# A hybrid decoder step on one core: convolution blocks earlier and further apart, LayerNorm beside the last projections

## Chip, core and metric

The kernel runs on one core of one Trainium2 chip. The metric is the time of one execution in microseconds (us); 3151.36 is the median of three. A profile is one execution recorded by the hardware profiler. Engines are called PE (matrix products), DVE (vector), ACT (activations, scalar engine), POOL (GpSimd) and SP (sync engine, which issues most DMAs).

## The reference, cut

One layer over 2048 prompt rows and 32 sample rows (2080 columns in the kernel, which works on transposed data). All branches come from one projection of the normalized input:

```python
h = _rmsnorm(x, g_pre) @ w_in
qa, ka, va, za, ub, zb, qc, zc, gt = jnp.split(h, SPLITS, axis=-1)
...                                                # A: dilated attention of qa, ka, va
glu = ub[..., :EB] * jax.nn.sigmoid(ub[..., EB:])   # B: EB = 768
full = jnp.concatenate([hist_conv, glu], axis=1)
conv = lax.conv_general_dilated(full, conv_w[:, None, :], ..., feature_group_count=EB) + conv_b
ob = jax.nn.silu(_layernorm(conv, ln_g, ln_b))      # width 31; norm over 768 channels
...                                                # C: cross-attention of qc into 256 memory rows
mix = (gates[..., 0, :] * ((oa * jax.nn.silu(za)) @ w_pa)
       + gates[..., 1, :] * ((ob * jax.nn.silu(zb)) @ w_pb)
       + gates[..., 2, :] * ((oc * jax.nn.silu(zc)) @ w_pc))
y = x + _rmsnorm(mix @ w_out, g_post)
```

## The kernel before

**Stages.** First x is loaded, normalized and transposed in six groups of columns (`stage_x`), split into a high and a low part (x0h, x0l and so on), and two weight blocks q0 and q1 are multiplied chunk by chunk as x arrives. Then come the other projections of this stage, one block for each 128 output columns. A block loads its weights (`load_w`), splits them on POOL into `whi` and `wlo` (L55, L56), and runs 144 matmuls on PE into the PSUM tile `g` (L166 to L168): 6 chunks of columns (384 wide, then 256 and 288) by 8 row blocks by 3 products. Then the memory stage (`memory`: keys and values of the memory rows, the LayerNorm, cross-attention), the sample's attention, the prompt's attention, and a last stage that projects the branches and the output. A further set of projections (za, zb, zc, gt; PSUM tile `gg`) has low priority and fills gaps of PE from the end of the first projections until after attention; it is called the filler below.

**Blocks.** k and v blocks copy chunks to `st` (ACT), transpose them on PE and copy them to `ro` on DVE (L260, L264) for the outputs. q and qc blocks only store `st`. A u block is two weight blocks: the gate (tanh on ACT into `gate`) and the values, whose chunks DVE joins with the gate into `G` (prompt) and `GS` (sample) at L298 and L303. The order before is u0, k0, k1, k2, u1, k3, k4, k5, u2 and so on: each u with three others, q2 to q5 and qc0 to qc3 among the last.

**Convolution.** After each u block, `conv` takes 31 taps on DVE: L313 writes the accumulator `acc` (one buffer), L322 adds the other taps, L331 and L333 handle the sample. Then `acc` is stored to `d_c` (L335, SP). It is put off by 900 in priority (`later(LAG)`), so that it fills DVE beside the blocks that follow.

**LayerNorm.** `conv_norm` is a generator with one step for each of 9 chunks of 256 columns: load from `d_c` (L663), sum over six channel blocks (L665, DVE), sum over partitions by a product with `ones` on PE (L667, tile `str`), subtraction (L668), squares on ACT (L671), their sum (L673), again a product (L675, tile `sco`), variance (L677), root, scaling (L679, and POOL at L681), tanh on ACT (L684), product (L685), store. `memory_kv` takes a step after each of its eight weight blocks. The norm has pools of its own there.

**Order.** A scheduler gives each engine one fixed instruction order from priorities, its own estimates of times, and free buffers. On the chip every engine takes its list strictly in order, and waits at an instruction whose inputs are not there.

Of the kernel before, what the change touches and what calls it, by code (L numbers as in the profile page):

```python
# [7 lines left out]
F32 = mybir.dt.float32  # L8
R32 = mybir.dt.float32r
AF = mybir.ActivationFunctionType  # L10
ALU = mybir.AluOpType
# [14 lines left out]
LAG = 900  # L26
EARLY = 1
IN_COLS = 9472

# [8 lines left out]
class K:  # L38
# [134 lines left out]
    def phase_a1(self, wp, blocks=None):  # L173
        tc, nc, I, O = self.tc, self.nc, self.I, self.O
        with tc.tile_pool(name="x12", side="right", bufs=1) as xpool, \
                tc.tile_pool(name="stg", side="right", bufs=3) as stg, \
                tc.tile_pool(name="sm1", side="right", bufs=2) as small, \
                tc.tile_pool(name="wr", side="right", bufs=2) as self.wr, \
                tc.tile_pool(name="psg", side="right", bufs=4, space=PSUM, reuse_waits="tile") as psg, \
                tc.tile_pool(name="pst", side="right", bufs=3, space=PSUM, reuse_waits="tile") as pst:  # L180
            for th in (1, 2):
                n = THIRDS[th][1]
                self.X[th] = tuple([xpool.tile([128, n], R32, name=f"x{th}{c}{k}") for k in range(8)]
                                   for c in "hl")
            with tc.tile_pool(name="xst", side="right", bufs=7) as xst:
                st = self.stage_x(xst, small, pst)
                next(st)
                self.consts(self.cpool, xst, pst)
                ws = [self.load_w(wp, self.win(CQ), 8, rp=self.wr)]
                for _ in st:  # L190
                    pass
            with tc.tile_pool(name="brw", side="right", bufs=1) as bp:
                self.taps(self.cpool, bp, pst)
                self.bias_rows(self.cpool, bp, pst)

            out = [(th, c, k) for th in (1, 2) for c in range(2) for k in range(8)]

            with tc.tile_pool(name="cnv", side="right", bufs=1, reuse_waits="tile") as cnv:
                ws.append(self.load_w(wp, self.win(CQ + 128), 8, rp=self.wr))
                for cs, js in [(c, j) for c in (CHUNKS[:1], CHUNKS[1:2], CHUNKS[2:3], CHUNKS[3:4], CHUNKS[4:]) for j in range(2)]:  # L200
                    for s, n in cs:
                        self.chunk("q", js, s, n, ws[js], stg, psg, "g", pst)
                order = []
                rest = [("k", j) for j in range(6)] + [("v", j) for j in range(6)] + \
                       [("q", j) for j in range(2, 6)] + [("qc", j) for j in range(4)]
                for j in range(6):
                    order += [("u", j)] + rest[:3]
                    rest = rest[3:]
                order += rest
                for kind, j in order:  # L210
                    if blocks is not None and (kind, j) not in blocks:
                        continue
                    if kind == "u":
                        gs = self.blk_u(j, wp, stg, cnv, psg, pst)
# [7 lines left out]
                assert not out  # L222
                self.early = {("za", j): self.load_w(wp, self.win(CZA + 128 * j), 8, rp=self.wr) for j in range(EARLY)}
    def blk_x(self, kind, j, wp, stg, psg, pst):
# [42 lines left out]

    def blk_u(self, j, wp, stg, cnv, psg, pst):
        nc, I, O = self.nc, self.I, self.O
        G = cnv.tile([128, 16, 130], F32, name="G", bufs=2)  # L270
        GS = cnv.tile([128, 8, 34], F32, name="GS", bufs=2)
        nc.gpsimd.memset(G[:, :, 0:2], 0.0)
# [7 lines left out]
        for x in range(2):  # L280
            nc.vector.tensor_scalar(GS[:, 4 * x:4 * x + 4, 0:30],
                                    p[:, x * 128:x * 128 + 120].rearrange("p (b w) -> p b w", b=4),
                                    2.0, None, op0=ALU.mult)

        w = self.load_w(wp, self.win(CUB + EB + j * 128), 8, rp=self.wr)
        gate = cnv.tile([128, T], F32, name="gate")
# [5 lines left out]
        for s, n in CHUNKS:  # L292
            th = gate[:, s:s + n]
            pa = psg.tile([128, 512], F32, name="g")
            self.gemm(pa[:, :n], w, [self.x_at(k, s, n) for k in range(8)])
            m = min(n, S - s)
            r0 = s // 128
            nc.vector.scalar_tensor_tensor(G[:, r0:r0 + m // 128, 2:130],  # L298
                                           th[:, :m].rearrange("p (r i) -> p r i", i=128), 1.0,
                                           pa[:, :m].rearrange("p (r i) -> p r i", i=128),  # L300
                                           op0=ALU.add, op1=ALU.mult)
            if m < n:
                nc.vector.scalar_tensor_tensor(GS[:, :, 30:34],  # L303
                                               th[:, m:n].rearrange("p (b t) -> p b t", t=4), 1.0,
                                               pa[:, m:n].rearrange("p (b t) -> p b t", t=4),
                                               op0=ALU.add, op1=ALU.mult)
        return G, GS

# [345 lines left out]

    def conv_norm(self, lp, ps):
        nc = self.nc
        ones = lp.tile([128, 128], F32, name="ones")
        nc.vector.memset(ones, 1.0)
        W = 256
        for s in range(0, T, W):  # L660
            n = min(W, T - s)
            x = lp.tile([128, 6, W], F32, name="c", bufs=3)[:, :, :n]
            nc.sync.dma_start(x, self.d_c[:, :, s:s + n].rearrange("j p n -> p j n"))  # L663
            sm = lp.tile([128, W], F32, name="sm", bufs=2)[:, :n]
            nc.vector.tensor_reduce(sm, x.rearrange("p j n -> p n j"), axis=AX.X, op=ALU.add)  # L665
            p = ps.tile([128, 512], F32, name="str")[:, :n]
            nc.tensor.matmul(p, ones, sm, start=True, stop=True)  # L667
            nc.vector.scalar_tensor_tensor(x, p[:, None, :].to_broadcast([128, 6, n]), -1.0 / EB, x,  # L668
                                           op0=ALU.mult, op1=ALU.add)
            sq = lp.tile([128, 6, W], F32, name="sq", bufs=1)[:, :, :n]  # L670
            nc.scalar.activation(sq, x, AF.Square)  # L671
            sm = lp.tile([128, W], F32, name="sm", bufs=2)[:, :n]
            nc.vector.tensor_reduce(sm, sq.rearrange("p j n -> p n j"), axis=AX.X, op=ALU.add)  # L673
            p = ps.tile([128, 512], F32, name="sco")[:, :n]
            nc.tensor.matmul(p, ones, sm, start=True, stop=True)  # L675
            var = lp.tile([128, W], F32, name="var")[:, :n]
            nc.vector.tensor_scalar(var, p, 1.0 / EB, EPS, op0=ALU.mult, op1=ALU.add)  # L677
            rs = self.rsqrt(lp, var, [128, W], "ln", n)
            nc.vector.tensor_tensor(x, x, rs[:, None, :].to_broadcast([128, 6, n]), op=ALU.mult)  # L679
            for j in range(6):  # L680
                nc.gpsimd.tensor_scalar(x[:, j], x[:, j], self.v("ln_g", j), self.v("ln_b", j),  # L681
                                        op0=ALU.mult, op1=ALU.add)
            t = lp.tile([128, 6, W], F32, name="sq", bufs=1)[:, :, :n]
            nc.scalar.activation(t, x, AF.Tanh, scale=0.5)  # L684
# [199 lines left out]
    def memory(self):  # L884
        tc = self.tc
        with tc.tile_pool(name="mem", side="right", bufs=1, reuse_waits="tile") as kp, \
                tc.tile_pool(name="ln", side="right", bufs=1, reuse_waits="tile") as lp, \
                tc.tile_pool(name="lnp", side="right", bufs=1, space=PSUM, reuse_waits="tile") as lps:
            ln = self.conv_norm(lp, lps)
            with tc.tile_pool(name="mem1", side="right", bufs=1, reuse_waits="tile") as mp, \  # L890
                    tc.tile_pool(name="mem1p", side="right", bufs=2, space=PSUM, reuse_waits="tile") as ps, \
                    tc.tile_pool(name="memw", side="right", bufs=2, reuse_waits="tile") as wp:
                KT, VV = self.memory_kv(mp, kp, wp, ps, ln)
            for _ in ln:
                pass
            with tc.tile_pool(name="mem2", side="right", bufs=1, reuse_waits="tile") as mp, \
# [7 lines left out]

    def memory_kv(self, mp, kp, wp, ps, ln):
        nc, I, O = self.nc, self.I, self.O
# [22 lines left out]
        for c in range(8):  # L929
# [18 lines left out]
            if c >= 4:  # L948
# [3 lines left out]
                VV.append((vh, vl))  # L952
            next(ln, 0)
        return KT, VV
# [353 lines left out]
```

## Time and profile before

| | |
|---|---|
| median of 3 runs (lowest to highest) | 3151.36 us (3148.8 to 3155.62) |
| the profiled execution, its own time | 3154.4 us |
| its span in the profile | 3152.6 us |
| mean granted clock of PE | 0.979 |
| PE, DVE, POOL, ACT busy | 3000.2, 2014.8, 1350.4, 1124.2 us |
| first projections end (last matmul into `g`) | 868.6 us |
| filler (matmuls into `gg`) | 868.7 to 2549.7 us |
| starts of the six convolutions | 154.1, 274.0, 394.2, 514.4, 634.6, 754.9 us |

The page gives, for each engine, busy time and its share of the span; the chain that ended last; and groups of instructions by line. Since each engine works in order, one asks in each stretch which engine is never idle, and, where PE is idle, what it waited for.

### The profile page before, as it was taken

How to read it: one execution, taken by the hardware profiler on the slowest of the kernel's cores; microseconds unless marked ns; L12 is line 12 of the kernel's file. 1: busy time of each engine (PE TensorE's matmuls, PEld its weight loads, DVE VectorE, ACT ScalarE, POOL GpSimd, SP SyncE). 2: the span in 40 equal slices, each digit the busy share in tenths (PEclk: the TensorE clock that was granted, in tenths of full speed). 3: DMA queues.
4: the chain of work that ended last, by engine and by line, in shares of the span. 5: the costliest groups of instructions: out<-in, count | busy, mean ns of one | idle time of the engine just before them, and what ended most of it. 6: DMA issues, size and time to landing. Idle time of an engine off the chain costs nothing.

```text
span 3152.6 us, 55374 instructions
## 1 busy us (share of the span) xinstructions
PE 3000.2 (95%) x20705; PEld 2839.9 (90%) x20705; DVE 2014.8 (64%) x3734; ACT 1124.2 (36%) x2835; POOL 1350.4 (43%) x1048
## 2 busy tenths in 40 slices
PE   7999999999987999999999999989899979999998
PEld 6899999999987999998999999989898967787897
DVE  5297797796677926465546766666656457556563
ACT  5010010010132433243437575656565523222221
POOL 0121221142356537444256565667676433233240
PEclk9899999999999999999999999999999989999999
DMA  7232222211265454477454656576555487657561
GB/s 250 85 103 80 80 60 61 63 62 50 81 182 167 135 153 144 147 219 239 151 139 116 161 123 163 128 185 150 156 143 152 109 279 227 223 168 227 161 197 53
DMA packets 532218, 454.66 MB, mean 144 GB/s; under 512 B 118191, under 2 KB 458581, under 8 KB 531137
## 3 DMA queue, kind: packets, MB, share of 16 engines
q1 hardware_dynamic: 357502, 335.36, 36.2%
q10 hardware_dynamic: 169840, 105.02, 11.7%
q0 software_dynamic: 4608, 10.75, 1.2%
q8 instruction: 164, 2.69, 0.4%
q14 instruction: 104, 0.85, 0.1%
HBM read 332.96 MB, written 118.04 MB: 143 GB/s over the span
## 4 chain that ended last, share of the span: by engine, by line
PE 70%; DMA 12%; DVE 7%; issue 4%; POOL 3%; ACT 2%; SPq 1%; ACTq 0%; DVEq 0%; POOLq 0%
PE g L166 8%; PE g L167 8%; PE g L168 8%; PE gg L166 6%; PE gg L168 6%; PE gg L167 6%; PE pg L168 3%; PE pg L166 3%; PE pg L167 3%; PE pt L571 2%; DMA cb<-d_cf 2%; PE y L1180 2%; PE y L1179 2%; PE y L1178 2%; PE o L598 1%
## 5 line engine op out<-in xcount | busy, mean ns | idle before, releaser
L166 PE MATMUL gg<-x0h,whi 128*128 128x256 f32 (+1 forms) x2560 | 747.9, 292 | 25.9 <-DVE st L246 12.2
L168 PE MATMUL gg<-x0h,wlo 128*128 128x256 f32 (+1 forms) x2560 | 741.8, 290 | 0.1
L167 PE MATMUL gg<-x0l,whi 128*128 128x256 f32 (+1 forms) x2560 | 741.1, 290 | 0.0
L55 POOL TENSOR_SCALAR whi<-wraw 128x1024 fp32r<-128x1024 f32 x162 | 242.7, 1500 | 928.5 <-PE g L167 524.1
L166 PEld LDWEIGHTS gg<-x0h,whi 128*128 128x128 f32 x2560 | 493.2, 193 | 35.0 <-DVE st L246 13.7
L167 PEld LDWEIGHTS gg<-x0l,whi 128*128 128x128 f32 x2560 | 493.5, 193 | 2.2 <-issue 0.5
L168 PEld LDWEIGHTS gg<-x0h,wlo 128*128 128x128 f32 x2560 | 493.2, 193 | 2.2 <-POOL wlo L56 0.3
L322 DVE SCALAR_TENSOR_TENSOR acc<-G,cw,acc 128x1536 f32<-128x1536 f32 (+15 forms) x354 | 480.8, 1408 | 0.3
L56 POOL TENSOR_TENSOR wlo<-wraw,whi 128x1024 fp32r<-128x1024 f32 x162 | 417.0, 2575 | 9.4 <-PE gg L168 0.2
L155 POOL TENSOR_TENSOR clo<-craw,chi 128x768 fp32r<-128x768 f32 (+1 forms) x96 | 174.1, 1815 | 346.0 <-ACT chi L154 329.8
L627 ACT ACTIVATE P<-T,stm 128x128 f32<-128x128 f32 (+1 forms) x576 | 260.8, 455 | 141.0 <-DVE stm L625 94.8
L239 ACT ACTIVATE st<-g 128x384 f32<-128x384 f32 (+1 forms) x132 | 60.2, 461 | 570.7 <-PE g L168 550.7
L166 PE MATMUL pg<-ac,chi 128*128 128x512 f32 (+1 forms) x640 | 229.4, 359 | 16.6 <-ACT chi L154 8.7
L625 DVE CUSTOM_DVE_ANT_0 T<-s,bias 128x128 f32<-128x128 f32 (+1 forms) x576 | 191.5, 357 | 80.8 <-PE s L617 47.0
L167 PE MATMUL pg<-ac,chi 128*128 128x512 f32 (+1 forms) x640 | 228.8, 358 | 6.3 <-DVE ac L1198 6.3
L168 PE MATMUL pg<-ac,clo 128*128 128x512 f32 (+1 forms) x640 | 227.6, 357 | 3.6 <-POOL clo L155 3.6
L576 DVE TENSOR_TENSOR pl<-pt,ph 128x512 fp32r<-128x512 f32 x240 | 155.6, 652 | 52.4 <-ACT ph L575 48.9
L168 PE MATMUL g<-x0h,wlo 128*128 128x384 f32 x544 | 184.3, 339 | 2.9 <-POOL wlo L56 2.9
L166 PE MATMUL g<-x0h,whi 128*128 128x384 f32 x544 | 183.6, 338 | 2.6 <-ACT st L239 2.3
L167 PE MATMUL g<-x1l,whi 128*128 128x384 f32 x544 | 186.0, 342 | 0.0
L167 PE MATMUL g<-x0l,whi 128*128 128x384 f32 x544 | 185.8, 342 | 0.0
L168 PE MATMUL g<-x1h,wlo 128*128 128x384 f32 x544 | 185.8, 342 | 0.0
(330 smaller groups left out, 7425.0 us busy)
## 6 DMA issues: line engine op xcount, KB each, us to landing
wraw<-in_w_in ACTq DMA_DIRECT2D x119, 512.0 KB
d_g<-st ACTq DMA_DIRECT2D x168, 128.0 KB
cb<-d_cf SPq DMA_DIRECT2D x72, 256.0 KB
g<-d_g SPq DMA_DIRECT2D x72, 256.0 KB
wraw<-in_w_in SPq DMA_DIRECT2D x35, 512.0 KB
kvc<-in_cache_k_win SPq DMA_DIRECT2D x8, 1536.0 KB
kvc<-in_cache_v_win SPq DMA_DIRECT2D x8, 1536.0 KB
raw<-d_q SPq DMA_DIRECT2D x48, 256.0 KB
```

The lines of the kernel that those rows point to most:

```text
L55: nc.gpsimd.tensor_scalar(hi, raw, 1.0, 1.0, op0=ALU.mult, op1=ALU.mult)
L56: nc.gpsimd.tensor_sub(lo, raw, hi.bitcast(F32))
L155: nc.gpsimd.tensor_sub(lo, raw, hi.bitcast(F32))
L166: nc.tensor.matmul(ps, hi[:, k, :], h, start=k == 0, stop=False)
L167: nc.tensor.matmul(ps, hi[:, k, :], l, start=False, stop=False)
L168: nc.tensor.matmul(ps, lo[:, k, :], h, start=False, stop=k == kb - 1)
L322: nc.vector.scalar_tensor_tensor(a3[:, lo:hi], G[:, src:src + hi - lo, 2 - m:130 - m], w, a3[:, lo:hi], op0=ALU.mult, op1=ALU.add)
L571: nc.tensor.transpose(t[:, 128 * x:128 * x + 128], pc, self.ident)
L576: nc.vector.tensor_tensor(pl[:, :w], t[:, :w], ph[:, :w].bitcast(F32), op=ALU.subtract)
L625: nc.vector.tensor_tensor_reduce(sc[:, :w], t[:, o:o + w], bias[:, 256 - w:256], 1.0, 3.0e38, ALU.add, ALU.min, m)
L627: nc.scalar.activation(P[:, o:o + w], sc[:, :w], AF.Exp, bias=m, scale=-1.0, accum_out=self.stl[:, col:col + 1])
L1178: nc.tensor.matmul(y[:m, c, :], ah[:, ts_], bh[:, cs], start=k == 0, stop=False)
```

## The change

It has five parts. (1) The chunks that go with the staging of x are no longer q0 and q1 but the gate and the values of u0; the gate's tanh goes to `st` there, and one of the two pairs of `G` and `GS` moves to a pool that is opened earlier (`cng`), while the x buffers go from 7 to 6. (2) After that the order is u1, k0, k1, u2, k2, k3 and so on: two other blocks to a u; q0 to q5 and qc0 to qc3 come last. (3) The transposes of the sample's state are a function of their own (`states`), and the zeroing of `G`'s edge goes with the first chunk of values. (4) The norm's steps are taken after each of the twelve blocks behind u5's two, with a priority 800 ahead of them; they are no longer in the memory stage. (5) The norm uses the convolution's buffers: x in `G`, sums in `GS`, squares and tanh in `gate`, rows in `acc`, and the PSUM tile `tr` of the row transposes; the two reductions over six become adds, and the root is written out.

```diff
+AHEAD = 800
...
-            with tc.tile_pool(name="xst", side="right", bufs=7) as xst:
+            g0 = ctx.enter_context(tc.tile_pool(name="cng", side="right", bufs=1, reuse_waits="tile"))
+            with tc.tile_pool(name="xst", side="right", bufs=6) as xst:
...
-                ws.append(self.load_w(wp, self.win(CQ + 128), 8, rp=self.wr))
-                for cs, js in [(c, j) for c in (CHUNKS[:1], CHUNKS[1:2], CHUNKS[2:3], CHUNKS[3:4], CHUNKS[4:]) for j in range(2)]:
-                    for s, n in cs:
-                        self.chunk("q", js, s, n, ws[js], stg, psg, "g", pst)
+                self.gpools = (g0, cnv)
+
+                ws.append(self.load_w(wp, self.win(CUB), 8, rp=self.wr))
+                first = self.gated(0)
+                for s, n in CHUNKS:
+                    pb = psg.tile([128, 512], F32, name="g")
+                    self.gemm(pb[:, :n], ws[0], [self.x_at(k, s, n) for k in range(8)])
+                    th = stg.tile([128, 384], F32, name="st")
+                    nc.scalar.activation(th[:, :n], pb[:, :n], AF.Tanh, scale=0.5)
+                    self.values(*first, s, n, ws[1], th, psg)
...
-                       [("q", j) for j in range(2, 6)] + [("qc", j) for j in range(4)]
+                       [("q", j) for j in range(6)] + [("qc", j) for j in range(4)]
                 for j in range(6):
-                    order += [("u", j)] + rest[:3]
-                    rest = rest[3:]
+                    order += [("u", j)] + (rest[:2] if j else [])
+                    rest = rest[2:] if j else rest
                 order += rest
+                ln = self.conv_norm(cnv, pst)
...
+                    if (kind, j) in rest:
+                        with self.later(-AHEAD):
+                            next(ln, 0)
...
+        if s == 0:
+            nc.gpsimd.memset(G[:, :, 0:2], 0.0)
...
-            nc.vector.tensor_reduce(sm, x.rearrange("p j n -> p n j"), axis=AX.X, op=ALU.add)
-            p = ps.tile([128, 512], F32, name="str")[:, :n]
+            sm = GS.rearrange("p b w -> p (b w)")[:, :n]
+            nc.vector.tensor_add(sm, x[:, 0], x[:, 1])
+            for j in range(2, 6):
+                nc.vector.tensor_add(sm, sm, x[:, j])
+            p = ps.tile([128, 512], F32, name="tr")[:, :n]
             nc.tensor.matmul(p, ones, sm, start=True, stop=True)
...
-            nc.vector.tensor_reduce(sm, sq.rearrange("p j n -> p n j"), axis=AX.X, op=ALU.add)
-            p = ps.tile([128, 512], F32, name="sco")[:, :n]
-            nc.tensor.matmul(p, ones, sm, start=True, stop=True)
+            nc.vector.tensor_add(sq[:, 0:3], sq[:, 0:3], sq[:, 3:6])
+            nc.vector.tensor_add(sq[:, 0], sq[:, 0], sq[:, 1])
+            nc.vector.tensor_add(sq[:, 0], sq[:, 0], sq[:, 2])
+            p = ps.tile([128, 512], F32, name="tr")[:, :n]
+            nc.tensor.matmul(p, ones, sq[:, 0], start=True, stop=True)
+            rows = cnv.tile([128, T], F32, name="acc")
...
-            next(ln, 0)
```

The second of these removed `next(ln, 0)` stood in `memory_kv`. Line numbers shift: the matmuls are L167 to L169 in the changed kernel, the row copies L278 and L282, values L328 and L333, the first tap L342, the others L351, the norm's sums L702 and L704, its products L706 and L715.

What this does to the fixed orders shows at two places. First PE around the first two products of the norm. Before, they stand among filler matmuls, the second some thirty rows behind the first:

```order
L166 MATMUL gg<-x0h_192,whi 128x256
L167 MATMUL gg<-x0l_200,whi 128x256
L667 MATMUL str<-sm,ones 128x256
L168 MATMUL gg<-x0h_192,wlo 128x256
L166 MATMUL gg<-x0h_193,whi 128x256
L167 MATMUL gg<-x0l_201,whi 128x256
```

Now, at the end of q0's first chunk (`trc` is the conv state's transpose of block 5, `tr<-ident,st` the row transposes of v5, and the `g` behind them q0's next chunk):

```order
L168 MATMUL g<-x0l_201,whi 128x384
L169 MATMUL g<-x0h_193,wlo 128x384
L372 MATMUL trc<-ident,so 30x128
L374 MATMUL trc<-ident,so 120x128 x2
L706 MATMUL tr<-GS,ones 128x256
L715 MATMUL tr<-gate,ones 128x256
L274 MATMUL tr<-ident,st 128x128 x12
L167 MATMUL g<-x0h_186,whi 128x384
```

Both products of the first chunk now stand directly one behind the other, ahead of twelve transposes and the remaining q and qc blocks.

Second DVE between two convolutions. Before, the values of the next u block stand there:

```order
L322 SCALAR_TENSOR_TENSOR acc<-G,cw,acc 128x256
L322 SCALAR_TENSOR_TENSOR acc<-G,cw,acc 128x1792
L298 SCALAR_TENSOR_TENSOR G<-gate,g 128x3x128 x4
L298 SCALAR_TENSOR_TENSOR G<-gate,g 128x2x128 x2
L303 SCALAR_TENSOR_TENSOR GS<-gate,g 128x8x4
L313 TENSOR_SCALAR acc<-G,cw,vecs 128x2048
```

Now, as in this piece in the middle of a convolution, they stand among the taps:

```order
L351 SCALAR_TENSOR_TENSOR acc<-G,cw,acc 128x640
L328 SCALAR_TENSOR_TENSOR G<-gate,g 128x3x128
L351 SCALAR_TENSOR_TENSOR acc<-G,cw,acc 128x1280
L351 SCALAR_TENSOR_TENSOR acc<-G,cw,acc 128x768
L351 SCALAR_TENSOR_TENSOR acc<-G,cw,acc 128x1152
L328 SCALAR_TENSOR_TENSOR G<-gate,g 128x3x128
```

and ahead of the norm's first sum DVE has taps of convolution 5 with nothing else among them, of which these are the last:

```order
L351 SCALAR_TENSOR_TENSOR acc<-G,cw,acc 128x384
L351 SCALAR_TENSOR_TENSOR acc<-G,cw,acc 128x1664
L351 SCALAR_TENSOR_TENSOR acc<-G,cw,acc 128x256
L351 SCALAR_TENSOR_TENSOR acc<-G,cw,acc 128x1792
L702 TENSOR_TENSOR GS<-G 128x256
```

The values moved from between the convolutions into them, and the norm's first sum directly follows the last tap.

More of the change, by code (lines that the diff above doesn't have):

```diff
@@ L1 @@
-from contextlib import contextmanager
+from contextlib import ExitStack, contextmanager
 import numpy as np
@@ L213, in phase_a1 @@
                     if kind == "u":
-                        gs = self.blk_u(j, wp, stg, cnv, psg, pst)
+                        gs = first if j == 0 else self.gated(j)
+                        self.states(j, cnv, pst, gs[1])
+                        if j:
+                            self.blk_u(j, wp, cnv, psg, *gs)
                         with self.later(LAG):
@@ L292, in blk_u, with values @@
         for s, n in CHUNKS:
[L293 to L300, printed above, removed]
-                                           op0=ALU.add, op1=ALU.mult)
[L302 to L307, printed above, removed]
+            self.values(G, GS, s, n, w, gate[:, s:s + n], psg)
+    def values(self, G, GS, s, n, w, th, psg):
+        nc = self.nc
+        pa = psg.tile([128, 512], F32, name="g")
+        self.gemm(pa[:, :n], w, [self.x_at(k, s, n) for k in range(8)])
+        m = min(n, S - s)
+        r0 = s // 128
+        if s == 0:
+            nc.gpsimd.memset(G[:, :, 0:2], 0.0)
+        nc.vector.scalar_tensor_tensor(G[:, r0:r0 + m // 128, 2:130],
+                                       th[:, :m].rearrange("p (r i) -> p r i", i=128), 1.0,
+                                       pa[:, :m].rearrange("p (r i) -> p r i", i=128),
+                                       op0=ALU.add, op1=ALU.mult)
+        if m < n:
+            nc.vector.scalar_tensor_tensor(GS[:, :, 30:34],
+                                           th[:, m:n].rearrange("p (b t) -> p b t", t=4), 1.0,
+                                           pa[:, m:n].rearrange("p (b t) -> p b t", t=4),
+                                           op0=ALU.add, op1=ALU.mult)
     def conv(self, j, cnv, pst, G, GS):
@@ L682, in conv_norm @@
                                         op0=ALU.mult, op1=ALU.add)
-            t = lp.tile([128, 6, W], F32, name="sq", bufs=1)[:, :, :n]
+            t = six(cnv.tile([128, T], F32, name="gate"))
             nc.scalar.activation(t, x, AF.Tanh, scale=0.5)
@@ L903, in memory, with memory_kv @@
                     pass
[L905 removed]
+    def memory_kv(self, mp, kp, wp, ps):
         nc, I, O = self.nc, self.I, self.O
```

53 lines of the change are left out of this document (32 added, 21 removed).

## Prediction

> **What bounds the kernel now.** I read the page first, then a table of stretches, then the waits of the stretch that the change empties, then the rows of the engines that meet there. Rows 1 and 4 of the page:
>
> ```profile
> PE 3000.2 (95%) x20705; PEld 2839.9 (90%) x20705; DVE 2014.8 (64%) x3734; ACT 1124.2 (36%) x2835; POOL 1350.4 (43%) x1048
> PE 70%; DMA 12%; DVE 7%; issue 4%; POOL 3%; ACT 2%; SPq 1%; ACTq 0%; DVEq 0%; POOLq 0%
> ```
>
> TensorE (PE) is busy 95% of 3152.6 us and carries 70% of the chain. The number of matmuls and their sizes stay the same with the change, so the time can only move by what PE stands idle, or runs at a lower clock. Where it does now shows the table of stretches (columns: length; busy us and count of PE, PEld, DVE, ACT, POOL; granted clock; DMA):
>
> ```profile
> 0.00:100.00 100.00, 76.20 (x444) 67.41 (x445) 52.32 (x110) 50.08 (x102) 13.88 (x14) 0.92 0.70 245
> 274.00:394.20 120.20, 120.20 (x778) 119.65 (x777) 98.36 (x108) 11.05 (x24) 26.15 (x12) 1.00 0.28 87
> 650.00:700.00 50.00, 44.79 (x283) 44.06 (x281) 49.93 (x42) 5.54 (x12) 31.27 (x4) 1.00 0.21 66
> 860.00:1150.00 290.00, 253.24 (x1951) 244.62 (x1950) 208.39 (x276) 103.64 (x193) 156.61 (x143) 0.95 0.52 159
> 2520.00:2620.00 100.00, 79.59 (x408) 65.82 (x407) 60.29 (x71) 31.30 (x48) 39.23 (x23) 0.91 0.91 290
> ```
>
> The second row is one period of the projection stage: a u pair and three other blocks, 120.2 us, PE never idle, VectorE (DVE) busy 98.4. The convolution has 21.8 us to spare there. The fourth is the memory stage with the normalization: PE idle 36.8 us, and 5% of the clock, 14.5 us, gone beside it. What PE waits for there (total, times, longest):
>
> ```profile
> PE sco L675 <- DVE sm L673: 14.9, 5, 9.0
> PE gg L166 <- DVE st L246: 10.1, 9, 1.8
> PE str L667 <- DVE sm L665: 4.5, 5, 1.4
> ```
>
> and the longest of these on PE's timeline:
>
> ```profile
> 946.18 0.28 PE L168 MATMUL gg<-x0h,wlo 128*128 128x256 f32 x1
> 955.50 1.22 PE L675 MATMUL sco<-sm,ones 128*128 128x256 f32 x2 [9.04 <-DVE sm L673]
> 959.88 0.41 PE L166 MATMUL gg<-x0h,whi 128*128 128x256 f32 x1
> ```
>
> So the old norm costs about 20 us of direct waits, and after such a wait a filler matmul shows 0.41 us for 0.28.
>
> **The change: the convolution chain against PE.** Order now: u0 with the staging, then u1, k0, k1, u2, k2, k3 ... u5, v2, v3, then v4, v5, q, qc. A period is two u blocks and two k/v blocks. Block lengths come from the weight splits on GpSimd (POOL), one per block, each set off by PE:
>
> ```profile
> 177.85 1.67 POOL L55 TENSOR_SCALAR whi<-wraw 128x1024 fp32r<-128x1024 f32 x1 [19.97 <-PE g L167]
> 202.53 2.48 POOL L55 TENSOR_SCALAR whi<-wraw 128x1024 fp32r<-128x1024 f32 x1 [19.83 <-PE g L167]
> 708.44 1.05 POOL L55 TENSOR_SCALAR whi<-wraw 128x1024 fp32r<-128x1024 f32 x1 [19.93 <-PE g L167]
> 731.46 1.05 POOL L55 TENSOR_SCALAR whi<-wraw 128x1024 fp32r<-128x1024 f32 x1 [18.91 <-PE g L167]
> ```
>
> A k/v block takes 24.7 us (177.85 to 202.53), a u or q block about 22.9 (708.44 to 731.46: 23.0). PE's new period is 2 x 22.9 + 2 x 24.7 = 95.2 us. DVE's: 98.4 less the row copies of the one k/v block that leaves the period,
>
> ```profile
> L260 DVE COPY ro<-tr 128x384 f32<-128x384 f32 x12 | 6.5, 539 | 0.0
> L260 DVE COPY ro<-tr 128x256 f32<-128x256 f32 x6 | 2.5, 409 | 0.0
> L264 DVE COPY ro<-tr 32x128 f32<-32x128 f32 x3 | 0.8, 270 | 0.0
> ```
>
> a third of 9.8, so 98.4 - 3.2 = 95.1 us, and then a wait that is new. The accumulator `acc` has one buffer, and its store must land before the next convolution writes it. Before, the values of the next block hide this:
>
> ```profile
> 246.80 2.07 DVE L322 SCALAR_TENSOR_TENSOR acc<-G,cw,acc 128x1792 f32<-128x1792 f32 x1
> 254.89 0.56 DVE L298 SCALAR_TENSOR_TENSOR G<-gate,g 128x384 f32<-128x384 f32 x1 [6.02 <-PE g L168]
> 273.97 1.52 DVE L313 TENSOR_SCALAR acc<-G,cw,vecs 128x2048 f32<-128x2048 f32 x1
> ```
>
> The last tap ends at 249, the next convolution starts at 274. In the new order the values stand among the taps, and the next convolution's first tap follows almost on the last. The store itself shows no landing; the nearest row is the reload of 0.79 MB of the same data, 866.35 to 871.20, 4.9 us (rows below). Bounds 0 and 4.9 us a period; I take 4.0, since a few small operations still lie between. DVE's period is then 99.1 us, 4 us longer than PE's: DVE falls behind, which by itself PE does not feel.
>
> It feels it at the norm. In PE's new order the two matmuls of the first chunk (L706, L715) stand right behind q0's first chunk, ahead of v5's transposes and all that is left of q and qc. PE takes its queue in order, so it stands still until convolution 5 is done, stored, reloaded and summed. Rows for this (L313 starts, L335 stores; then load, sums, squares of the old norm's first chunk):
>
> ```profile
> L313 DVE TENSOR_SCALAR acc<-G,cw,vecs x6: 1519/1521/1522, 154.1 to 754.9; 128x2048 f32<-128x2048 f32 x6
> L335 SPq DMA_DIRECT2D d_c<-acc x6: 319/344/345, 248.9 to 839.4; - x6
> 859.36 0.17 DVE L658 MEMSET ones<- 128x128 f32 x1 [19.98 <-PE g L167]
> 866.35 0.40 SPq L663 DMA_DIRECT2D c<-d_c  x1
> 871.20 2.93 DVE L665 TENSOR_REDUCE sm<-c 128x256 f32<-128x1536 f32 x1 [0.71 <-DMA c<-d_c]
> 874.99 1.76 DVE L668 SCALAR_TENSOR_TENSOR c<-str,c 128x1536 f32<-128x1536 f32 x1 [0.85 <-PE str L667]
> 883.39 2.84 DVE L673 TENSOR_REDUCE sm<-sq 128x256 f32<-128x1536 f32 x1 [5.98 <-ACT sq L671]
> 888.87 0.42 DVE L677 TENSOR_SCALAR var<-sco 128x256 f32<-128x256 f32 x1
> L671 ACT ACTIVATE sq<-c x9: 364/1487/1491, 881.9 to 1125.0; 128x1536 f32<-128x1536 f32 x8, 128x192 f32<-128x192 f32 x1
> ```
>
> Before, this had cover: convolution 5 was stored at 839.4, and DVE then stood idle 20 us until PE was through. Counted from the start of convolution 0:
> - DVE: five periods 5 x 99.1 = 495.5; the last convolution 84.5 (754.9 to 839.4) and one row copy or two, 85.5; store 4.5 and reload 4.9 (estimates from 4.9); five adds of 256 columns by the 0.42 row, 2.1. First sum at +592.5. Then matmul, subtraction 1.76, square 1.49, three adds about 1.9 (by width from 0.42), matmul, with two matmuls at 0.8 and the hand-overs 8.5 together (in the old norm 12 us lie between the two matmuls, with reductions of 2.8). PE goes on at +601.
> - PE without a wait: u1 to u5, ten blocks, 229.0; twelve k/v blocks 296.4; q0's first chunk 384/2080 of 22.9, 4.2; less 1.3 for v5's twelve transposes that stand behind; less 10.6 for the two and a half chunks of u1's gate that the order has PE do before convolution 0 can start (it stands behind the bias rows' last copies on DVE). +517.7.
>
> The difference, **+83 us**, is lost. The visible stall may be smaller if PE is held earlier by row copies among the taps; the sum is the same. Bounds: 63 with the store wholly hidden (5 x 4 less), 104 at 98.4 + 4.9 a period. After the stall PE comes back at the lower clock: 14.5 us of lost clock for some five waits in the memory stage gives **+3**.
>
> **The other terms.**
> - Norm chunks beside q and qc: the order leaves just under a block, 20.5 us of products, from one chunk's first sum to the next's. One chunk is nearly serial, since `gate` holds its squares and its tanh: square 1.5, adds 1.9, matmul 0.8, variance 0.4, root with table load 1.7, reciprocal 1.75, four small ones 1.7, product 1.75, scaling on POOL 3.3, tanh with table load 2.8, last product 1.75, near 19.4, and 2 for hand-overs, 21.4. Eight times 0.9 is **+8** with rounding. The old norm took 28 us a chunk, which bounds it above at 8 x 7.5 = 60; below it is 0.
>
> ```profile
> 994.21 1.75 DVE lnr L64
> 933.71 3.26 POOL c L681 x6
> L685 DVE SCALAR_TENSOR_TENSOR c<-sq,c x9: 359/2439/12593, 908.9 to 1132.5; 128x1536 f32<-128x1536 f32 x8, 128x192 f32<-128x192 f32 x1
> ```
>
> - Staging of x: tanh of u0's gate now alternates with the square roots, nine more table loads in ScalarE's order, each as here:
>
> ```profile
> 8.34 1.28 ACT L63 ACT_TABLE_LOAD   x1
> 9.64 0.20 ACT L63 ACTIVATE rxs<-var 128x3 f32<-128x3 f32 x1
> ```
>
> 9 x 1.28 = 11.5 us on an engine that is busy 50 of the first 100 us, while PE idles 23.8 there, partly on ACT. I take **+4** (0 to 11.5), with the sixth instead of seventh x buffer in it. The Trainium skill's page "ScalarE: Activation LUTs", section "What ACT_TABLE_LOAD costs", adds a drain of about 1.38 us to each load, which would make this 24 us and the total some 4 us more at the same share. The trace disagrees: the next ACTIVATE starts 0.02 us after the load ends.
> - The gap at 683 goes, **-5**: the weight split at 657 took 21.74 us beside 25 taps in a row, in a q block without row copies, and PE waited 2.95 and 2.26 us (5.2 of the third stretch). Convolution 4 now runs beside v blocks.
>
> ```profile
> 657.08 21.74 POOL L55 TENSOR_SCALAR whi<-wraw 128x1024 fp32r<-128x1024 f32 x1 [18.76 <-PE g L167]
> 683.21 0.45 PE L168 MATMUL g<-x0h,wlo 128*128 128x384 f32 x1 [2.95 <-POOL wlo L56]
> 227.22 1.65 POOL L55 TENSOR_SCALAR whi<-wraw 128x1024 fp32r<-128x1024 f32 x1 [17.81 <-PE g L167]
> ```
>
> - The memory stage without the norm: the direct waits of 19.4 us and most of the 14.5 us of clock, **-33**. Bounds -15 (the `sco` waits alone) and -51 (all idle time and clock).
> - The rest of the filler is longer after attention, and phase C's first loads get cover: **-5** of the 20.4 idle in the last stretch (0 to -20).
> - Free: six sums as adds instead of a reduction (2.1 for 2.9), the memset in `values`, the state transposes; all on engines that wait for PE or inside the 83.
>
> Sum: 3154.4 + 83 + 3 + 4 + 8 - 5 - 33 - 5 = 3209.4 for the profiled execution, whose span is 3152.6. It stands 3 us above the median 3151.4, so the forecast is **3206 us**.
>
> **Rivals.**
> 1. Not slower. All that the memory stage loses comes back (51), all of the last stretch (20) and the 5, while the stall is at its lowest (63) and nothing else costs: 3154.4 + 63 - 76 = 3141, or 3138 by the median. It decides where the stall falls below the gains, 43 by my sum, less 15 of side costs: under 28, for which DVE's period would have to be 88 us against 98.4 measured with 9.8 of copies. Against it speaks that the filler, which could cover PE, stands behind in its order. 0.07; no change within 0.2% (about what a measurement of this kernel can tell) 0.03.
> 2. The norm's chunks run at the old 28 us: 60 for 8, **3258**. For it: the last product's mean of 2.4 us and once 12.6 while POOL splits weights. Against: in the old norm filler, memory and norm shared DVE. 0.12.
> 3. DVE slower still. Taps now meet the splits all the time: a tap row of 50 without a row copy stands ahead of the norm. At 103.3 us a period the loss is 104: **3227**. For it: 21.74 us at 657.08, where POOL and DVE delay each other; against: 1.65 at 227.22, in the gate block as it will be. The page "SBUF — State Buffer" of the Trainium skill, section "Who interferes with whom", calls the port pair shared by the two an exclusive lock; by that rule PE would also wait for weights in each period, five times 5.2 us, but before the norm such waits vanish in the 83. The trace agrees with the lock at 657.08 and not at 227.22. 0.13.
>
> **Chances and range.** My case, 3175 to 3225, 0.65; rivals as above. Slower by over 0.2%: 0.90. The range runs from 3160 (stall 63 with the memory stage at -45) to 3245 (104, or the chunks at 26 us).
>
> **What would show it.** Right: a single PE idle stretch of 60 to 85 us ending at L706 near 700 us, with taps L351 on DVE right through it; convolution starts 98 to 100 us apart with 3 to 4 us of DVE idle before L342; stretches of the memory stage with PE idle under 20; filler alone after attention. Wrong: PE idle before L706 under 30 us, convolution starts 95 us apart as PE's period, or chunks of the norm more than 24 us apart.

## The result: 1.6% slower, and the profile after

The changed kernel takes 3202.56 us (median of four, 3196.41 to 3211.05), beside 3150.08 for the kernel before: a ratio of 1.0163 (95% interval 1.0144 to 1.0183). The profiled execution took 3202.7 us, its span is 3200.9. Forecast were 3206.

Rows 1 and 4 of the page after:

```profile
PE 2995.9 (94%) x20705; PEld 2840.5 (89%) x20705; DVE 2007.7 (63%) x3788; ACT 1137.7 (36%) x2845; POOL 1304.3 (41%) x1048
PE 58%; DVE 19%; DMA 11%; issue 5%; POOL 4%; ACT 2%; SPq 1%; ACTq 0%; DVEq 0%; POOLq 0%
DVE acc L351 12%; PE gg L167 7%; PE gg L168 7%; PE gg L169 7%; PE pg L169 3%; PE pg L168 3%; PE pg L167 3%; PE g L167 3%; PE g L169 3%; PE g L168 3%; PE pt L600 2%; PE y L1221 2%; PE y L1220 2%; PE y L1219 2%; DMA rv<-out_v_win_p 2%
```

PE has the same 20705 matmuls and is busy 4.3 us less; the span is 48.3 us longer, so PE idles 52.6 us more. The convolution's taps (L351) now carry 12% of the chain; before, they were not among the lines that the page lists for it. Where the idle time lies shows the table of stretches. But for the first cut, at 150 us in both, they are cut at the same places of the program: staging, projections, memory stage, the sample's attention, attention with the filler's tail, last stage (columns as before: length; busy us and count of PE, PEld, DVE, ACT, POOL; clock; DMA). Before:

```profile
0.00:150.00 150.00, 126.20 (x714) 111.53 (x715) 58.23 (x122) 54.13 (x109) 17.33 (x16) 0.92 0.52 176
150.00:868.70 718.70, 713.49 (x4580) 710.44 (x4579) 569.79 (x590) 68.71 (x149) 189.10 (x64) 1.00 0.23 70
868.70:1338.80 470.10, 430.60 (x3393) 416.48 (x3391) 293.23 (x471) 161.06 (x355) 261.44 (x236) 0.97 0.51 155
1338.80:1534.80 196.00, 187.11 (x1404) 173.62 (x1405) 113.82 (x232) 84.37 (x189) 84.42 (x138) 0.98 0.68 212
1534.80:2551.80 1017.00, 975.41 (x7886) 958.70 (x7884) 627.72 (x1815) 594.99 (x1786) 625.22 (x500) 0.98 0.58 147
2551.80:3152.60 600.80, 567.42 (x2736) 469.12 (x2736) 351.99 (x507) 160.94 (x248) 172.92 (x94) 0.97 0.60 190
```

After:

```profile
0.00:150.00 150.00, 123.77 (x676) 107.03 (x676) 84.30 (x160) 62.26 (x111) 19.07 (x16) 0.92 0.48 163
150.00:966.00 816.00, 736.00 (x4653) 729.55 (x4652) 653.93 (x706) 121.13 (x200) 173.94 (x118) 0.95 0.27 82
966.00:1273.80 307.80, 300.62 (x2441) 293.48 (x2439) 162.94 (x373) 99.94 (x274) 180.18 (x156) 0.99 0.50 150
1273.80:1470.40 196.60, 191.85 (x1472) 179.46 (x1470) 108.75 (x216) 86.12 (x192) 77.94 (x124) 0.99 0.61 189
1470.40:2611.30 1140.90, 1079.94 (x8739) 1065.40 (x8737) 646.91 (x1836) 610.07 (x1824) 685.48 (x541) 0.97 0.57 149
2611.30:3200.90 589.60, 563.72 (x2736) 465.56 (x2736) 350.88 (x501) 158.22 (x246) 167.69 (x93) 0.98 0.60 187
```

PE's idle time in the six stretches (length less busy) was 23.8, 5.2, 39.5, 8.9, 41.6, 33.4 and is 26.2, 80.0, 7.2, 4.8, 61.0, 25.9 us. The projections lose 74.8, the memory stage gets 32.3 back, and attention loses 19.4, for which the forecast had no term.

Most of the loss in the projections is one wait, 61.2 of the 74.8 us. PE's timeline, and the waits of PE over the whole span that have the norm's products:

```profile
654.20 0.38 PE L374 MATMUL trc<-ident,so 128*120 128x128 f32 x2
715.82 1.19 PE L706 MATMUL tr<-GS,ones 128*128 128x256 f32 x2 [61.23 <-DVE GS L704]
722.37 1.19 PE L715 MATMUL tr<-gate,ones 128*128 128x256 f32 x2 [5.37 <-DVE gate L713]
PE tr L706 <- DVE GS L704: 67.2, 4, 61.2
```

PE comes to the norm's first product at 655, and stands there until 716 and again until 722. DVE, store and reload in the same time, and the wait for the accumulator's store at the start of a convolution:

```profile
693.72 11.11 DVE L351 SCALAR_TENSOR_TENSOR acc<-G,cw,acc 128x1280 f32<-128x1280 f32 x9
704.86 0.35 SPq L364 DMA_DIRECT2D d_c<-acc  x1
708.75 0.97 SPq L700 DMA_DIRECT2D G<-d_c  x2
713.41 0.42 DVE L702 TENSOR_TENSOR GS<-G 128x256 f32<-128x256 f32 x1 [8.57 <-DMA G<-d_c]
L342 DVE TENSOR_SCALAR acc<-G,cw,vecs x6: 1325/1346/1348, 121.6 to 621.9; 128x2048 f32<-128x2048 f32 x6
  DMA d_c<-acc: 19.2, 5
```

DVE runs taps until 704.9. Store and reload take 8.57 us until the first sum starts. The convolutions start every 100.1 us (121.6 to 621.9, five periods), and of each period 3.8 us are the wait for the store. So they stand earlier than before but closer together (100.1 us for 120.2), not further apart as the title says.

### The profile page after: what moved, and what is told of

Read it like the earlier page. It is cut to its first block, busy times and chain, and to the rows that moved or that the text cites. A ratio compares the mean times of both kernels' runs of the same rounds, so it can differ in the third digit from the quotient of the medians.

```text
span 3200.9 us, 55547 instructions
## 1 busy us (share of the span) xinstructions
PE 2995.9 (94%) x20705; PEld 2840.5 (89%) x20705; DVE 2007.7 (63%) x3788; ACT 1137.7 (36%) x2845; POOL 1304.3 (41%) x1048
## 4 chain that ended last, share of the span: by engine, by line
PE 58%; DVE 19%; DMA 11%; issue 5%; POOL 4%; ACT 2%; SPq 1%; ACTq 0%; DVEq 0%; POOLq 0%
DVE acc L351 12%; PE gg L167 7%; PE gg L168 7%; PE gg L169 7%; PE pg L169 3%; PE pg L168 3%; PE pg L167 3%; PE g L167 3%; PE g L169 3%; PE g L168 3%; PE pt L600 2%; PE y L1221 2%; PE y L1220 2%; PE y L1219 2%; DMA rv<-out_v_win_p 2%
## 5 line engine op out<-in xcount | busy, mean ns | idle before, releaser
L167 PE MATMUL gg<-x0h,whi 128*128 128x256 f32 (+1 forms) x2560 | 743.3, 290 | 20.2 <-DMA x0h<-d_x 10.5
L169 PE MATMUL gg<-x0h,wlo 128*128 128x256 f32 (+1 forms) x2560 | 739.3, 289 | 2.5 <-POOL wlo L57 2.5
L56 POOL TENSOR_SCALAR whi<-wraw 128x1024 fp32r<-128x1024 f32 x162 | 203.2, 1255 | 926.4 <-PE g L168 587.1
L167 PEld LDWEIGHTS gg<-x0h,whi 128*128 128x128 f32 x2560 | 492.4, 192 | 24.6 <-issue 11.3
L169 PEld LDWEIGHTS gg<-x0h,wlo 128*128 128x128 f32 x2560 | 492.4, 192 | 4.8 <-POOL wlo L57 2.8
L351 DVE SCALAR_TENSOR_TENSOR acc<-G,cw,acc 128x1536 f32<-128x1536 f32 (+15 forms) x354 | 487.1, 1424 | 0.2
L167 PE MATMUL pg<-ac,chi 128*128 128x512 f32 (+1 forms) x640 | 227.2, 357 | 13.8 <-ACT chi L155 7.0
L257 ACT ACTIVATE st<-g 128x384 f32<-128x384 f32 x132 | 60.6, 459 | 499.3 <-PE g L169 495.2
L169 PE MATMUL pg<-ac,clo 128*128 128x512 f32 (+1 forms) x640 | 226.7, 355 | 5.2 <-POOL clo L156 5.2
L169 PE MATMUL g<-x0h,wlo 128*128 128x384 f32 x544 | 188.0, 346 | 0.0
L167 PE MATMUL g<-x0h,whi 128*128 128x384 f32 x544 | 186.7, 345 | 1.2 <-POOL whi L56 0.8
L169 PE MATMUL g<-x1h,wlo 128*128 128x384 f32 x544 | 185.7, 342 | 0.0
L167 PE MATMUL g<-x1h,whi 128*128 128x384 f32 x544 | 182.3, 339 | 1.1 <-ACT x1h L136 1.1
```

The lines of the kernel that those rows point to most:

```text
L56: nc.gpsimd.tensor_scalar(hi, raw, 1.0, 1.0, op0=ALU.mult, op1=ALU.mult)
L167: nc.tensor.matmul(ps, hi[:, k, :], h, start=k == 0, stop=False)
L169: nc.tensor.matmul(ps, lo[:, k, :], h, start=False, stop=k == kb - 1)
L351: nc.vector.scalar_tensor_tensor(a3[:, lo:hi], G[:, src:src + hi - lo, 2 - m:130 - m], w, a3[:, lo:hi], op0=ALU.mult, op1=ALU.add)
```

## The experiments

The theory: PE's queue has the norm's first product ahead of work that could run, and DVE's chain of convolutions reaches the norm some 61 us later than PE (PE arrives at 655 and goes on at 716). Each group of runs has its own runs of the kernel before beside it (3155.12 us for the first four, 3151.97 for the last three); ratios refer to those. PE work per step is counted in columns; 2.2 thousand are about 1 us of a projection block.

**The norm begins three blocks later.**

```diff
-                    if (kind, j) in rest:
+                    if (kind, j) in rest[3:]:
```

> The norm's steps begin three blocks later (after q1 instead of after v4); nothing else changes. PE's order now has its first product 141 thousand columns further back, some 64 us of products. Theory (the loss is PE standing at the norm's first product, which stands in its queue ahead of v5's transposes and eleven blocks, until convolution 5 is through): of the 75 us of idle time around L706 about 10 remain, the time falls from 3202.6 to about 3137 us (3128 to 3150), the idle time of the memory stage stays near 7 us. Rival (convolutions and norm together on DVE bound the stage, so that the wait only moves to the end of the projections): PE idles some 60 us between the last projection and the memory stage, the time stays near 3195 to 3205 us.

Measured: 3153.74 us, ratio 0.9997 (0.998 to 1.0014). PE's timeline at the norm's first product and at the last chunk's second:

```profile
722.55 1.19 PE L706 MATMUL tr<-GS,ones 128*128 128x256 f32 x2 [7.46 <-DVE GS L704]
917.06 0.61 PE L715 MATMUL tr<-gate,ones 128*128 128x32 f32 x2 [16.11 <-DVE gate L713]
```

The wait of 61.2 us is 7.5, though the product itself starts 6.7 us later than in the changed kernel (722.6 beside 715.8): PE has done three blocks more by then. That bears the theory out; the rival, a stage bound by DVE wherever the norm stands, does not hold: behind the last projection PE idles 17 us, not 60. But the time is 17 us above the expectation, mainly because of the second row: 16.1 us ahead of the ninth chunk, which now stands behind the last projection with nothing in PE's queue that could cover it. The loss in attention stays too (61.0 us idle there, as after the change).

**The norm back in the memory stage**, with the rest of the change kept (`conv_norm`, `memory` and `memory_kv` as before, the steps after the projection blocks taken out):

```diff
-                    if (kind, j) in rest:
-                        with self.later(-AHEAD):
-                            next(ln, 0)
...
+            next(ln, 0)
```

> The norm goes back into the memory stage with its own buffers and reductions, as in the kernel before; u0 with the staging of x and two blocks to a u are kept. Theory: no stall at the norm, but the 32 us of waits in the memory stage and some clock come back: 3202.6 - 75 - 6 + 32 + 3, the time is about 3155 us (3142 to 3165), as the kernel before. Rival (the earlier and wider-spread convolutions cost by themselves, through the store of the accumulator or the staging of x): the time stays above 3180 us, with PE idle during the convolutions.

Measured: 3175.69 us, ratio 1.0068 (1.0045 to 1.009), between theory and rival. PE's waits in its memory stage are there again:

```profile
PE gg L167 <- DVE st L258: 10.3, 4, 5.7
PE str L690 <- DVE sm L688: 7.8, 6, 2.1
PE sco L698 <- DVE sm L696: 7.3, 4, 3.4
```

So moving the norm in the change's form costs about 30 us (1.0163 less 1.0068), and the rest of the change, the earlier convolutions with the new order of blocks, about 20. In the two profiles the span differs by 22.1 us: 5.8 are idle time of PE (158.2 against 152.4), the other 16.3 are PE's busy time (3016.5 against 3000.2) with the same 20705 matmuls, spread over the stages. The mean granted clock is 0.976 beside 0.979, which is worth about 9 of them as an estimate (0.3% of 3016). What in the new order does this stays open.

**A shorter last convolution** (15 of 31 taps of block 5 left out):

```diff
-        for sh in range(1, 31):
+        for sh in range(1, 31 if j < 5 else 16):
```

> The last convolution leaves out 15 of its 31 taps (results of that block are not the reference's); all orders stay. Its taps take some 85 us, so about 41 us less of DVE work ahead of the norm. Theory: the stall before L706 shrinks one for one, from 61 to about 20 us, and the time falls by 41 to about 3161 us (3152 to 3170). Rival (PE is held there by the buffers that the norm took, whose release does not hang on convolution 5, or the 61 us are made good later): the time stays within 10 us of 3202.6.

Measured: 3169.08 us, ratio 1.0057 (1.004 to 1.0075), 33 us less than the change, as the theory has it and not the rival.

```profile
679.27 1.19 PE L706 MATMUL tr<-GS,ones 128*128 128x256 f32 x2 [26.17 <-DVE GS L704]
```

The product comes 36.5 us earlier (679.3 beside 715.8), and the wait is 35 us shorter. Nearly every microsecond of convolution 5 is a microsecond of the kernel there. The 41 us expected were some 5 too many: two instructions make a tap, and undisturbed they take 2.47 us in the changed kernel's trace, 37 us for 15 taps,

```profile
225.68 2.47 DVE L351 SCALAR_TENSOR_TENSOR acc<-G,cw,acc 128x1920 f32<-128x1920 f32 x2
```

where I had put 15/31 of the whole convolution, with the sample's part and the row copies in it.

**A PSUM tile of its own for the norm's products:**

```diff
-                tc.tile_pool(name="psg", side="right", bufs=4, space=PSUM, reuse_waits="tile") as psg, \
+                tc.tile_pool(name="psg", side="right", bufs=3, space=PSUM, reuse_waits="tile") as psg, \
...
-            p = ps.tile([128, 512], F32, name="tr")[:, :n]
+            p = ps.tile([128, 512], F32, name="nm", bufs=1)[:, :n]
```

> The norm's two products get a PSUM tile of their own (one bank, taken from the four of the projections' tile g, which has three left), instead of the tile tr of the row transposes; the norm's priority and the block after which it starts stay as in the change. PE's order then has v5's transposes and two and a half q blocks ahead of the first product, which moves 134 thousand columns back. Theory in its narrow form (not the priority as such but the norm's claim on the transposes' tile put it ahead of v5): the stall shrinks to about 10 us and the time is about 3140 us (3130 to 3155). Rival 1 (the priority alone does it): the stall stays near 61 us, the time near 3200. Rival 2 (three banks are too few for the projections): small waits of PE on ACT at each group, 0.2 us for each of 132 groups behind, 3165 to 3180 us.

Measured: 3159.82 us, ratio 1.0018 (1.0006 to 1.0031).

```profile
723.04 1.22 PE L706 MATMUL nm<-GS,ones 128*128 128x256 f32 x2 [5.78 <-DVE GS L704]
923.85 0.60 PE L715 MATMUL nm<-gate,ones 128*128 128x32 f32 x2 [16.28 <-DVE gate L713]
PE g L167 <- DVE G L328: 9.7, 11, 2.7
```

With the norm's rank and start untouched, the order and the wait change as in the first run, and the last chunk lies bare as there. The last row is the price of three banks: PE now waits 9.7 us in the projections for DVE to read a group's values, where the rival had ACT. The time lies 5 us above the expected range; the theory had neither the bare last chunk (16.3) nor this wait. No run took a bank from `g` alone, but the wait that this causes is a different one from that at L706.

**The rank taken away alone:**

```diff
-AHEAD = 800
+AHEAD = 0
```

> Only AHEAD is 0 instead of 800: the norm no longer ranks ahead of the projections. PE's order has the first product at the same place. Theory (what put the product there is the claim on the tile tr, not the rank): within 10 us of the changed kernel, a ratio to the kernel before of 1.013 to 1.019, the idle time before L706 stays at 55 to 65 us. Rival (the rank is what costs): the stall falls below 30 us and the ratio below 1.008.

Measured: 3211.02 us, ratio 1.0185 (1.0166 to 1.0204).

```profile
715.09 1.19 PE L706 MATMUL tr<-GS,ones 128*128 128x256 f32 x2 [61.34 <-DVE GS L704]
```

The same wait to a tenth of a microsecond. The rank in priority is not what costs; together with the run before it, the claim on `tr` is: once the norm's steps are written behind v4, its two products hold two of the three buffers that v5's transposes need, and the order lets v5 and all behind it wait for them. This last step is read from the program and the order; no run varied the number of buffers.

**q0 and q1 with the staging of x again** (the first part of the change undone, two other blocks to every u; the norm as in the change):

```diff
-                ws = [self.load_w(wp, self.win(CUB + EB), 8, rp=self.wr)]
+                ws = [self.load_w(wp, self.win(CQ), 8, rp=self.wr)]
...
-                    order += [("u", j)] + (rest[:2] if j else [])
+                    order += [("u", j)] + rest[:2]
```

> The first part of the change alone is undone: q0 and q1 go with the staging of x again, u0 behind it, two other blocks to every u; the norm runs beside the last projections as in the change. The convolutions begin about 45 us later, and in PE's order the first product of the norm stands at 1614 thousand columns (1400 in the change), with four of nine chunks behind the last projection. Theory: the wait before the first product falls under 15 us, but the last four chunks lie bare behind the projections, 16 us each as the one in the run begun three blocks later: 60 us idle there, a ratio of about 1.010 (1.004 to 1.017), and the staging of x loses the 2 us that it had gained. Rival (filler covers the bare chunks): a ratio of 1.000 or below.

Measured: 3190.61 us, ratio 1.0126 (1.01 to 1.0151).

```profile
746.87 1.19 PE L701 MATMUL tr<-GS,ones 128*128 128x256 f32 x2 [6.60 <-DVE GS L699]
911.60 1.19 PE L710 MATMUL tr<-gate,ones 128*128 128x256 f32 x2 [19.80 <-DVE gate L708]
922.76 1.22 PE L701 MATMUL tr<-GS,ones 128*128 128x256 f32 x2 [9.97 <-DVE GS L699]
932.69 1.19 PE L710 MATMUL tr<-gate,ones 128*128 128x256 f32 x2 [8.71 <-DVE gate L708]
939.64 0.64 PE L701 MATMUL tr<-GS,ones 128*128 128x32 f32 x2 [5.75 <-DVE GS L699]
949.20 0.60 PE L710 MATMUL tr<-gate,ones 128*128 128x32 f32 x2 [8.92 <-DVE gate L708]
```

As expected, the wait before the first product (first row) falls to 6.6 us, and the chunks that fall behind the last projection lie bare, 53 us of waits in the other five rows, with no filler to cover them. Two things differ here together: the convolutions start later (the first at 158.9 for 121.6, 37 us and not 45; the last at 640.4 for 621.9), and only eight blocks are left behind u5 where the change has twelve. So the first part of the change gives the norm more projections to stand beside; which of the two does more, this run does not tell.

**A version that beats both.** The norm begun three blocks later, in eight chunks of 260 columns, so that none is left over:

```diff
-                    if (kind, j) in rest:
+                    if (kind, j) in rest[3:]:
...
-        W = 256
+        W = 260
```

> As the run with the norm begun three blocks later (3153.7 us beside 3155.1 of the kernel before), and the norm takes eight chunks of 260 columns instead of eight of 256 and one of 32. That run's trace still had PE idle 16.1 us ahead of the ninth chunk's second product, after the last projection, where nothing else stood in its queue. Theory: this wait goes, since the eighth chunk's products now stand ahead of the last projections: 3153.7 - 14 = about 3140 us, a ratio to the kernel before of about 0.9955. Rival (the wait is that for the buffers that the memory stage takes over from the projections, whichever chunk is last): the idle time stays at the start of the memory stage, within 4 us of 3153.7.

Measured: 3142.74 us, ratio 0.9964 (0.995 to 0.9978), 9 us faster than the kernel before.

```profile
724.36 1.21 PE L706 MATMUL tr<-GS,ones 128*128 128x260 f32 x2 [7.20 <-DVE GS L704]
911.80 0.41 PE L966 MATMUL tr<-ident,mt 128*128 128x128 f32 x2 [3.88 <-DVE mt L962]
901.00:1211.00 310.00, 292.86 (x2365) 286.63 (x2366) 168.29 (x388) 100.67 (x276) 183.94 (x166) 0.97 0.50 151
902.20:1211.00 308.80, 295.50 (x2363) 286.61 (x2363) 165.64 (x380) 98.97 (x272) 182.80 (x160) 0.98 0.51 154
1405.00:2546.80 1141.80, 1092.88 (x8802) 1076.84 (x8800) 640.90 (x1832) 611.51 (x1824) 689.16 (x543) 0.97 0.57 149
```

The third row is the memory stage of the run with nine chunks, the fourth that of this one, the fifth attention here. The wait at the last chunk is gone, but others came in its place (3.9 us in the second row, then for weights and for ACT): the memory stage idles 13.3 us for 17.1, a gain of 3.8 and not of 14, which in this stage fits the rival better. PE idles 48.9 us in attention here, 12 less than in the run with nine chunks, which was not expected. So the time came out as forecast in good part by luck: PE idles 22.2 us less in all (133.8 for 156.0, with 10.4 us more busy time beside it), and the stage that the edit aimed at gives only 3.8 of them. The kernel is faster than the one before; why attention gains is not shown.

## Why the prediction was right, step by step

- **The stall, +83 and +3 for the clock.** From the first convolution's start at 121.6, DVE starts its first sum at +591.8 and has it at +594.0 (forecast +592.5, with the adds), and PE goes on at about +602 (+601). This side was right to 1.5 us, partly because errors met: five periods of 100.1 us for 99.1 made it 5 us later, a last convolution of 83.0 us for 85.5 and store and reload of 8.57 for 9.4 made it 3 us earlier; the store wait was 3.8 for 4.0. On PE's side I had put it 9 us too far ahead. On PE the loss shows as 74.0 us of idle time up to the second product: 61.2 and 5.4 in the rows above, and 7.4 earlier, where row copies among the taps held it,

```profile
PE tr L301 <- DVE ro L278: 3.8, 2, 1.9
PE tr L274 <- DVE ro L278: 3.6, 3, 1.8
700.00:750.00 50.00, 28.82 (x163) 27.64 (x164) 29.90 (x43) 13.08 (x17) 6.15 (x8) 0.72 0.39 128
300.00:350.00 50.00, 48.08 (x297) 47.77 (x296) 46.00 (x52) 3.56 (x8) 10.27 (x5) 0.97 0.24 75
```

(waits of PE from 150 to 650, the stretch with the stall's end, and one with a wait among the taps). The clock of 0.72 means half speed up to about 728 (0.51 from 722 to 728, 1.00 from 728 to 735), some 7 us of products and 3 us of loss, as forecast. 77 of the 86 us are thus seen. Of the other 9 about 3 are clock lost before the norm: it was 0.97 from 300 to 350 and from 400 to 450, behind one wait of 1.9 us each. The rest is work of PE ahead of the norm that took longer than I had summed it from block lengths.
- **Norm chunks, +8:** PE idles 6.0 us from 724 on to the end of the projections. Both sides of this term were too short: from the third chunk on the first sums start 24.5 us apart (746.4 to 868.9, five steps), where I had 21.4 for a chunk and 20.5 for PE's work. That is just over the 24 us that I had named as a sign of being wrong. It did not cost what I feared, since PE had work in most of that time.
- **Staging, +4:** 2.4 us of idle time (26.2 for 23.8), with eight more table loads in the first 150 us (11 for 3), not nine. The ScalarE rows stand as the trace of before had them, with no drain behind a load:

```profile
30.98 1.28 ACT L210 ACT_TABLE_LOAD   x1
32.28 0.49 ACT L210 ACTIVATE st<-g 128x384 f32<-128x384 f32 x1
```

- **The gap at 683, -5:** gone; from 150 to 966 PE nowhere waits for POOL. The long weight split did come back, at 650 and shorter, inside the stall, where it costs nothing:

```profile
650.05 12.44 POOL L56 TENSOR_SCALAR whi<-wraw 128x1024 fp32r<-128x1024 f32 x1 [20.62 <-PE g L168]
```

- **Memory stage, -33:** 39.5 us of idle time became 7.2, -32.3, of which the term had 19.4 as waits and the rest as clock. The clock did rise there, from 0.97 to 0.99, but over the whole span PE's busy time fell by 4.3 us only: in attention the clock went from 0.98 to 0.97.
- **Last stage, -5:** 7.5 us of idle time less.
- **Missing: attention, +19.4 of idle time.** This step had no term; I took the filler's part there as moved and not changed. In the trace the filler's reload of x is not covered at one place, and some 18 us behind it PE waits for POOL:

```profile
1561.25 0.55 PE L167 MATMUL gg<-x0h,whi 128*128 128x256 f32 x1 [10.09 <-DMA x0h<-d_x]
1579.83 0.79 PE L429 MATMUL pt<-pl,perm 128*128 128x512 f32 x1 [5.56 <-POOL pl L57]
```

Before, PE waited 1.6 us for this reload during attention. The two rows are 15.7 us, most of the 19.4. No run here varied them alone: with the norm begun later and nine chunks the loss in this stretch is as large, with shorter waits of other kinds in their place, and with eight chunks it is 7 us. Why the filler meets attention worse in some orders stays open. That the forecast of 3206 came only 3 us off is partly luck. This unlisted loss of 19 us stands against a projection stage that lost 11 us less idle time than its terms (74.8 for 83 + 8 - 5), and against staging, the sample's attention and the last stage, 8 us better together than theirs. The stall itself, its cause and its place were forecast and came.

The rivals: not slower did not come, since the stall was nowhere near 28 us. The old pace of 28 us a chunk did not come: the pace was 24.5, and PE waited only 6 us. DVE was 1 us a period slower than forecast (100.1 us for 99.1), not 4 as in that rival (103.3). What I said against that rival, that DVE and POOL do not delay each other at 227.22, was read too fast: the split of 1.65 us there is 0.6 us longer than the 1.05 of others, and the two tap instructions from 228.35, beside it and the split's second half, take 4.92 us where two elsewhere take 2.47.

Two more slips in the working do not touch the sum. The ends of the range, 3160 and 3245, lie wider than the terms named for them, which give 3174 (20 and 12 below 3206) and 3242 (the chunks at 26 us; the 104 gives 3227). And the 2.4 us of the norm's last product is the median of its row, not the mean.

## What to carry to other kernels

Work that is moved to run beside other work is placed by the buffers that it shares as much as by its rank: a product that takes the tile of the transposes stands in the queue where those transposes stood, and an engine that works in order then waits for the whole chain behind it. Before such a move, time the chain that feeds it (here six convolutions at 100 us) against the moment at which the busy engine arrives, and begin the moved work that much later. Then look at its end: a chunk that falls behind the last block that could cover it made PE wait 16 us here, even one of 32 columns. Sizing the chunks without a remainder took that wait away, but the stretch as a whole gained only 3.8 us, so measure the stretch and not the one wait.

## What the runs showed of the hardware

After 61 us without a matmul PE ran at half clock (0.51) only to about 728, 12 us from its first product at 715.8, 5.4 of them idle: some 3 us of loss, little beside the stall itself. And the length of a weight split on POOL beside taps that follow one another on DVE can't be told from one row. It took 12.44 us at 650 in the changed kernel, and in the kernel before 21.74 at 657, 7.79 at 777, 1.40 at 800 and 17.29 at 823, where others take 1 to 4 us.
